# The products that complete a solve, alternating between the two directions of the scan

## Chip, cores and metric

The kernel runs on one core of one Trainium2 chip. The metric is the device time of one execution in microseconds (us): 3263.63 us is the median of three runs before the change (3262.67 to 3264.2). TensorE (PE in the rows, PEld for its weight loads), VectorE (DVE), ScalarE (ACT), GpSimd (POOL) and the DMA queues work side by side and wait for each other by semaphores.

## What is computed

Two layer stacks after each other on 512 tokens of width 1024 in fp32: a gMLP layer and an RWKV layer, each followed by a mixture of experts, then a sliding-window/dilated attention layer and a latent attention layer. The change lies in the RWKV layer's scan, which runs over 256 context tokens and 512 tokens, in two directions, for 16 heads of 64:

```python
def _wkv_step(S, inp):
    r_t, w_t, k_t, v_t, a_t, b_t = inp
    sa = jnp.einsum('zbhvk,zbhk->zbhv', S, a_t)
    S = S * w_t[..., None, :] + sa[..., :, None] * b_t[..., None, :] + v_t[..., :, None] * k_t[..., None, :]
    return S, jnp.einsum('zbhvk,zbhk->zbhv', S, r_t)

def wkv_bidir(state0, scan_in):
    state, ys = lax.scan(_wkv_step, state0, scan_in)
    ys = jnp.moveaxis(ys, 0, 2)
    return state, ys[0] + ys[1][:, ::-1]
```

## The kernel before

**The scan.** `rwkv_scan` works on 8 pairs of heads (`KD` = 8, index c), and cuts the 768 tokens into 12 chunks of 64 (`NCH` = 12, `C` = 64). Index z is the direction, h the head of the pair. Inside a chunk the steps are a triangular system, so its inverse has to be found: for each c a **solve** finds it for all 12 chunks, both directions and both heads at once. Then the **chain** (`Chain.period`) goes through the 12 chunks of the pair, one chunk a period, and carries the state from one to the next.

**A solve.** `scan_decay` and `scan_scaled` prepare its operands: decays and scaled keys in `BK` (line 1363 and 1369) and `AD` (line 1366), of which there are two copies each, used in turn by even and odd c, and 32 by 32 blocks of the system in `MT` (diagonal blocks) and `MO` (off-diagonal blocks). `solve` (line 1415 on) inverts the diagonal blocks on VectorE in 31 steps of two operations (`sol`, `Xx`), and writes the result in two layouts, `XR` (line 1436) and `XL` (line 1437), and parts of it into `XF` (line 1443). The off-diagonal block of the inverse is the product of three 32 by 32 blocks: `solve_v` forms the first product (tile `pv`, copied to `Vs`), `solve_x` the second (tile `px`, copied to `XF`). Both call `products`.

**`products`** holds, for each half b of the 12 chunks, one tile `ps` of one PSUM bank with 6 chunks. For every chunk and direction there is one fp32 matmul: 32 partitions in, 64 columns of weights, 64 moving columns. In `pv` the operands of direction 0 stand on partitions 0 to 31 and those of direction 1 on 64 to 95; in `px` on 32 to 63 and 96 to 127. Direction 0 writes partitions 0 to 63 of the bank, direction 1 partitions 64 to 127. So a call has 24 matmuls in four groups of 6 (half 0 direction 0, half 0 direction 1, half 1 direction 0, half 1 direction 1), and the trace has two records for each, 48 in all. When a half is done, ScalarE copies it out in four copies (line 1461).

**A period of the chain.** Its stages are `py` (tile `pY`), `pg` (`pG`), `pa` (`pA`), `ps` (`pS`) and `pz`, each for another chunk ahead; in the trace a period of one of the later 8 chunks of a pair is 36 records from `pY` to `pz`.

**What sets the order.** `todo` in `rwkv_scan` says before which period each step of the next pair's preparation is written: `solve` one period before the pair's first chunk is through, `solve_v` at its ninth period and `solve_x` at its tenth. Within one engine a scheduler orders the instructions by a simulated time line; the chain's matmuls, and from solve 1 on those of `products`, go through `R.pe = ch.pe`, an `Ordered` engine, whose instructions keep the order in which they are written. In solve 0, before the chain begins, `R.pe` is the plain engine.

**After the scan** come the RWKV layer's output projection (`rwkv_out`), a router that sorts the tokens for the second mixture of experts (`moe`; weights `we`, `wx` by the SyncE queue), the attention layer (`swa`) and the latent attention layer (`mla`).

Of the kernel before, what the change touches and what calls it, by code (L numbers as in the profile page):

```python
# [1445 lines left out]
def q(b):  # L1446
    return slice(32 * b, 32 * b + 32)


def products(K, R, name, lhs, rhs, out):  # L1450

    nh = NCH // 2
    for b in range(2):
        ps = R.q.tile([P, nh, 2, 32], F32, name=name, tag=R.tq[1 - b], bufs=2 if b else R.nq)
        for z in range(2):
            for i in range(nh):
                j = b * nh + i
                R.pe.matmul(ps[z * C:(z + 1) * C, i], lhsT=lhs(z, j), rhs=rhs(z, j), start=True, stop=True)
        for z in range(2):
            for h in range(2):  # L1460
                K.nc.scalar.copy(out(z, h, slice(b * nh, (b + 1) * nh)), ps[q(2 * z + h), :, h, :])
# [6 lines left out]
def solve_v(K, R, c, S):  # L1468

    S.V = V = R.s4.tile([P, NCH, 2, 32], F32, name="Vs")  # L1470
    products(K, R, "pv", lambda z, j: S.MO[q(2 * z), 2 * j:2 * j + 2].rearrange("p h t -> p (h t)"), lambda z, j: pair(S.XR, 2 * z, j),
             lambda z, h, js: V[q(2 * z + 1), js, h])


def solve_x(K, R, c, S):

    products(K, R, "px", lambda z, j: S.V[q(2 * z + 1), j].rearrange("p h t -> p (h t)"), lambda z, j: pair(S.XL, 2 * z + 1, j),
             lambda z, h, js: S.XF[q(2 * h), z, js, q(2 * h + 1)])
# [930 lines left out]
```

## Time and profile before

| | |
|---|---|
| median of three runs | 3263.63 us |
| the profiled execution | 3263.15 us |
| its span, first to last instruction | 3261.3 us |
| mean granted TensorE clock in it | 0.948 |
| TensorE busy | 2975.5 us, 91% of the span |
| VectorE busy | 1507.1 us, 46% |
| ScalarE busy | 1029.7 us, 32% |
| the scan, first `pv` to the last `pY` | 1437.06 to 2069.9 us |

All rows come from the one profiled execution; times in them are microseconds from the start of its span. A busy engine is one with an instruction in flight, so overlapping matmuls count once; several matmul records can be in flight at the same time. The granted clock is given as a share of 2.4 GHz: 1.00 is 2.4 GHz and 0.50 is 1.2 GHz. In the names, `pv<-XR,MO` is an instruction that writes `pv` and reads `XR` and `MO`; numbers of buffers are left out.

### The profile page before, as it was taken

What the parts mean: (1) busy time and instruction counts of PE and PEld (TensorE: products, weight loads), DVE (VectorE), ACT (ScalarE), POOL (GpSimd) and SP (SyncE); (2) the same over time, 40 slices, a digit from 0 to 9 for tenths busy, and PEclk for the clock granted to TensorE, in tenths of its full rate; (3) what the DMA queues carried; (4) which work ended last, traced back from release to release, by engine and by line L of the source; (5) the groups of instructions that cost most, each with busy time, mean ns of one, the idle gap of its engine ahead of it and who ended that gap; (6) DMA issues with size and microseconds to landing.
All of it is one profiled execution on the core that took longest, in us unless ns stands there. A gap on an engine that the chain in (4) does not pass through costs nothing. (4 is left out here: it accounts for less than half of the span.)

```text
span 3261.3 us, 51448 instructions
## 1 busy us (share of the span) xinstructions
PE 2975.5 (91%) x19312; PEld 2105.7 (65%) x19312; DVE 1507.1 (46%) x3441; ACT 1029.7 (32%) x2318; POOL 369.5 (11%) x456
## 2 busy tenths in 40 slices
PE   8999997999999799967999999889999978899998
PEld 4777786555545378646777778755554536777866
DVE  4342345010000399677787885441111125665584
ACT  4111231111111343254555554310000014544463
POOL 1022323111111100000000000021111110000000
PEclk9999998999999899978898999989999998999999
DMA  7545515899999814121111101569999993221200
GB/s 282 183 174 199 203 49 223 294 408 407 406 405 405 312 63 145 58 75 33 38 39 38 39 23 37 193 272 400 408 407 405 403 342 122 59 71 66 72 33 33
DMA packets 222834, 637.66 MB, mean 196 GB/s; under 512 B 37778, under 2 KB 65250, under 8 KB 222448
## 3 DMA queue, kind: packets, MB, share of 16 engines
q1 hardware_dynamic: 180048, 565.13, 45.6%
q10 hardware_dynamic: 27472, 45.72, 4.2%
q0 software_dynamic: 15056, 23.41, 2.0%
q8 instruction: 156, 2.56, 0.3%
q14 instruction: 102, 0.84, 0.1%
HBM read 609.24 MB, written 49.00 MB: 202 GB/s over the span
## 5 line engine op out<-in xcount | busy, mean ns | idle before, releaser
L793 ACT ACTIVATE hg<-pg 128x256 f32<-128x256 f32 x86 | 33.0, 383 | 787.1 <-PE pg L1495 787.1
L794 DVE TENSOR_TENSOR hg<-hg,pu 128x256 f32<-128x256 f32 x86 | 36.2, 421 | 521.0 <-PE pu L1495 518.3
L71 DVE TENSOR_TENSOR wl<-wr,wh 128x1024 fp32r<-128x1024 f32 (+1 forms) x140 | 168.5, 1219 | 121.2 <-ACT wh L70 120.4
L141 PE MATMUL ps<-hT,wh 128*128 128x512 f32 (+1 forms) x496 | 188.3, 380 | 8.4 <-DVE q L1957 3.8
L142 PE MATMUL ps<-hT,wh 128*128 128x512 f32 (+1 forms) x496 | 183.8, 371 | 0.0
L143 PE MATMUL ps<-hT,wl 128*128 128x512 f32 (+1 forms) x496 | 183.6, 371 | 0.0
L70 ACT CAST wh<-wr 128x1024 fp32r<-128x1024 f32 (+1 forms) x140 | 141.3, 1041 | 126.3 <-PE ps L143 43.3
L1495 PE MATMUL pu<-wx,xT 128*64 128x256 f32 x1520 | 176.3, 380 | 4.7 <-DMA wx<-in_moe_wu 4.7
L1495 PE MATMUL pd<-wx,hT 128*64 128x512 f32 x704 | 161.8, 598 | 16.5 <-issue 6.8
L1495 PE MATMUL pg<-wx,xT 128*64 128x256 f32 x1520 | 174.2, 379 | 1.1 <-DMA wx<-in_moe_wg 0.9
L764 DVE COPY hT<-pth 128x128 f32<-128x128 f32 x86 | 25.1, 291 | 312.3 <-ACT hT L763 308.6
L1495 PE MATMUL pd<-we,hT 128*64 128x512 f32 x672 | 154.8, 599 | 13.3 <-issue 8.4
L1495 PEld LDWEIGHTS pu<-wx,xT 128*64 128x64 f32 x1520 | 110.2, 137 | 83.9 <-issue 25.3
L734 POOL DMA_INDIRECT xe<-hrow,idx x86 | 88.3, 1026 | 652.5 <-PE ptr L1495 610.4
L1495 PE MATMUL pu<-we,xT 128*64 128x256 f32 x1232 | 143.2, 380 | 6.2 <-DMA we<-in_moe_wu 6.2
L1495 PE MATMUL pg<-we,xT 128*64 128x256 f32 x1232 | 144.9, 385 | 2.7 <-ACT xT L746 1.2
L1495 PEld LDWEIGHTS pg<-wx,xT 128*64 128x64 f32 x1520 | 111.5, 137 | 55.0 <-issue 2.1
L158 POOL TENSOR_TENSOR rs_r<-rs_t,nhalf 128x1 f32<-128x1 f32 (+2 forms) x52 | 45.5, 877 | 788.1 <-DVE rs_t L156 727.4
L1495 PEld LDWEIGHTS pu<-we,xT 128*64 128x64 f32 x1232 | 88.8, 137 | 66.6 <-issue 16.4
L1495 PE MATMUL pG<-SCB,Zx 128*128 128x128 f32 (+1 forms) x768 | 119.0, 303 | 12.4 <-DVE SCB L1562 8.5
L1495 PEld LDWEIGHTS pg<-we,xT 128*64 128x64 f32 x1232 | 90.1, 139 | 50.6 <-issue 5.4
L1495 PEld LDWEIGHTS pG<-SCB,Zx 128*128 128x128 f32 x768 | 104.8, 211 | 18.9 <-ACT Zx L1572 8.3
(583 smaller groups left out, 6545.0 us busy)
## 6 DMA issues: line engine op xcount, KB each, us to landing
wx<-in_moe_wu SPq DMA_DIRECT2D x144, 512.0 KB
wx<-in_moe_wg SPq DMA_DIRECT2D x144, 512.0 KB
wx<-in_moe_wd SPq DMA_DIRECT2D x130, 512.0 KB
we<-in_moe_wd SPq DMA_DIRECT2D x126, 512.0 KB
we<-in_moe_wg SPq DMA_DIRECT2D x112, 512.0 KB
we<-in_moe_wu SPq DMA_DIRECT2D x112, 512.0 KB
w<-in_ada_w SPq DMA_DIRECT2D x96, 512.0 KB
wr<-in_ga_w_in SPq DMA_DIRECT2D x32, 512.0 KB
```

The costliest lines, as they stand in the source:

```text
L70: nc.scalar.copy(hi, x)
L71: nc.vector.tensor_tensor(out=lo, in0=x, in1=hi.bitcast(F32), op=OP.subtract)
L141: nc.tensor.matmul(ps, lhsT=a[0], rhs=b[0], start=start, stop=False, **kw)
L142: nc.tensor.matmul(ps, lhsT=a[0], rhs=b[1], start=False, stop=False, **kw)
L143: nc.tensor.matmul(ps, lhsT=a[1], rhs=b[0], start=False, stop=stop, **kw)
L158: nc.gpsimd.tensor_tensor(out=r, in0=t, in1=K.nhalf[:, :n], op=OP.pow)
L734: nc.gpsimd.indirect_dma_start(out=xe[i % 3], out_offset=None, in_=hhalf, in_offset=bass.IndirectOffsetOnAxis(ap=idx[:, u, 0, r:r + 1], ax ...
L764: nc.vector.tensor_copy(hT[:, 1], pt[:, 1])
L793: nc.scalar.activation(hg, pg, AF.Silu)
L794: nc.vector.tensor_tensor(out=hg, in0=hg, in1=pu, op=OP.mult)
L1495: r = f(*a, **kw)
```

## The change

In `products` the loop over the two directions becomes the inner one: for each chunk the matmul of direction 0 and then that of direction 1 are issued. The matmuls, their operands and the copies are the same.

```diff
     for b in range(2):
         ps = R.q.tile([P, nh, 2, 32], F32, name=name, tag=R.tq[1 - b], bufs=2 if b else R.nq)
-        for z in range(2):
-            for i in range(nh):
-                j = b * nh + i
+        for i in range(nh):
+            j = b * nh + i
+            for z in range(2):
                 R.pe.matmul(ps[z * C:(z + 1) * C, i], lhsT=lhs(z, j), rhs=rhs(z, j), start=True, stop=True)
         for z in range(2):
             for h in range(2):
```

On TensorE the call stands at the same place. These are the rows around the `pv` and the `px` of one solve in the changed kernel; those of the kernel before read word for word the same (a row groups instructions of one name, x24 being the 24 matmuls of a call):

```order
L1495 MATMUL pz<-SC_11277,XF_9952 128x128 x2
L1495 MATMUL pv<-XR,MO 64x64 x24
L1495 MATMUL pY<-SV,G 128x64 x4
L1495 MATMUL pG<-SCB,Zx_10662 128x128 x4
...
L1495 MATMUL pz<-SC_11316,XF_9952 128x128 x2
L1495 MATMUL px<-XL,Vs 64x64 x24
L1495 MATMUL pY<-SV,G 128x64 x4
```

Nothing moved between the rows; what is new is the order within the two rows of 24.

On VectorE the first difference comes after the scan, in the router of the second mixture of experts (`ptr` is a transposed token tile, `h2T` its copy, `lg` the logits, the other names are small steps of the sorting):

```order
 L416 CAST grp<-gi 128x3
-L394 COPY h2T<-ptr 128x512
 L417 TENSOR_TENSOR oh<-i_16786,grp 128x12
 L420 TENSOR_TENSOR el<-lg,oh 128x32 x3
 L422 TENSOR_REDUCE es<-el 128x24
+L394 COPY h2T<-ptr 128x512
 L425 MAX em<-es 128x8 x3
 L426 MAX_INDEX ei<-em,es 128x8 x3
```

The copy of the last token tile now stands behind the five small operations instead of ahead of them.

On TensorE the first difference comes in the attention layer, where projection matmuls (`ps`), scores (`pss`), transposes of the probabilities (`pt`) and their products with the values (`po`) are interleaved. Before:

```order
L1974 MATMUL pss<-kb,q 128x256 x8
L141 MATMUL ps<-hT,wh 128x512
...
L2068 MATMUL po<-PT,vb_21225 64x128 x6
L2054 MATMUL pt<-ident,e 128x128 x5
L1974 MATMUL pss<-kb,q 128x256 x8
L2054 MATMUL pt<-ident,e 128x128 x3
L142 MATMUL ps<-hT,wh 128x512
```

And with the change:

```order
L1974 MATMUL pss<-kb,q 128x256 x4
L143 MATMUL ps<-hT,wl 128x512
L1974 MATMUL pss<-kb,q 128x256 x4
L2054 MATMUL pt<-ident,e 128x128
L2068 MATMUL po<-PT,vb_21225 64x128 x6
L2054 MATMUL pt<-ident,e 128x128 x7
L141 MATMUL ps<-hT,wh 128x512
```

The scores are cut into groups of four around a projection matmul, and the transposes stand together.

## Rows read from the trace of the kernel before

**Rows 1.** Windows: length; busy (instructions) of PE PEld DVE ACT POOL; granted clock; DMA.

```profile
1520.00:1600.00 80.00, 72.29 (x604) 60.66 (x604) 64.36 (x144) 45.70 (x118) 3.84 (x6) 0.91 0.13 39
...
1995.00:2078.00 83.00, 77.97 (x552) 65.20 (x550) 32.47 (x89) 39.34 (x102) 3.65 (x7) 0.92 0.18 62
```

**Rows 2.** Waits in the scan: who on whom, us in total, times, longest.

```profile
PE pv L1495 <- DVE XR L1436: 30.6, 6, 11.5
...
DVE BK L1363 <- PE pS L1495: 22.7, 6, 4.5
...
DVE AD L1366 <- PE pA L1495: 17.6, 6, 3.3
```

**Rows 3.** Timeline of TensorE in solve 2: start, us, instruction, records, [idle before].

```profile
1600.21 4.44 PE L1495 MATMUL pv<-XR,MO 32*64 32x64 f32 x48 [4.14 <-DVE XR L1436]
1604.58 1.97 PE L1495 MATMUL pY<-SV,G 128*128 128x64 f32 x8
...
1611.41 4.25 PE L1495 MATMUL px<-XL,Vs 32*64 32x64 f32 x48
1615.59 1.74 PE L1495 MATMUL pY<-SV,G 128*128 128x64 f32 x8
```

**Rows 4.** Timeline of VectorE after the px of solve 1.

```profile
1537.41 0.42 DVE L1602 TENSOR_TENSOR SV<-pY,WL 64x256 f32<-64x256 f32 x1 [2.09 <-PE pY L1495]
...
1541.95 0.96 DVE L1363 SCALAR_TENSOR_TENSOR BK<-ta,L 128x768 f32<-128x768 f32 x1 [3.51 <-PE pS L1495]
```

**Rows 5.** The SyncE queue right after the scan, then a window of the experts.

```profile
2068.13 8.99 SPq L130 DMA_DIRECT2D wr<-in_rw_wo  x4
...
2300.00:2400.00 100.00, 93.51 (x712) 55.59 (x708) 15.12 (x35) 9.18 (x27) 17.32 (x17) 1.00 1.03 408
```

**Rows 6.** TensorE's groups in the scan: records, busy us, mean ns, idle before.

```profile
L1495 PE MATMUL pv<-XR,MO 32*64 32x64 f32 x336 | 30.9, 290 | 30.6 <-DVE XR L1436 30.6
L1495 PE MATMUL px<-XL,Vs 32*64 32x64 f32 x336 | 29.7, 284 | 0.0
```

**Rows 7.** Timeline, pieces of the pv of solve 1: start, us, records.

```profile
1520.48 0.51 PE L1495 MATMUL pv<-XR,MO 32*64 32x64 f32 x3
...
1521.15 0.58 PE L1495 MATMUL pv<-XR,MO 32*64 32x64 f32 x6
...
1521.04 0.69 PE L1495 MATMUL pv<-XR,MO 32*64 32x64 f32 x7
```

**Rows 8.** Windows of 10 ns in that pv: the first (x) is records in flight.

```profile
1520.75:1520.76 0.01, 0.01 (x3) 0.01 (x2) 0.00 (x0) 0.50 0.00 0
...
1521.40:1521.41 0.01, 0.01 (x5) 0.01 (x4) 0.00 (x0) 0.50 0.00 0
```

**Rows 9.** Timeline of TensorE before the loop: the px of solve 0.

```profile
1443.52 4.44 PE L1458 MATMUL px<-XL,Vs 32*64 32x64 f32 x48 [2.04 <-ACT Vs L1461]
```

**Rows 10.** Timeline of ScalarE after the pv of solve 1.

```profile
1525.39 2.58 ACT L1461 COPY Vs<-pv 32x192 f32<-32x192 f32 x8
```

**Rows 11.** Windows, one period each: after px (two of seven), undisturbed, sum after pv.

```profile
1536.27:1542.53 6.26, 6.26 (x35) 4.92 (x35) 1.58 (x4) 2.33 (x7) 0.00 (x0) 0.73 0.26 86
1615.59:1623.45 7.86, 7.86 (x36) 6.49 (x36) 1.58 (x4) 2.34 (x7) 0.00 (x0) 0.57 0.23 69
...
2042.90:2047.44 4.54, 4.54 (x36) 3.88 (x35) 1.13 (x3) 2.47 (x8) 0.00 (x0) 1.00 0.12 33
...
sum 50.73, PE 50.73 PEld 41.26 DVE 14.63 ACT 33.31 POOL 0.00; mean PE 7.25 PEld 5.89 DVE 2.09 ACT 4.76 POOL 0.00
```

**Rows 12.** Windows of the px of solve 1 and of what follows it.

```profile
1532.10:1536.20 4.10, 4.10 (x49) 3.99 (x48) 3.16 (x5) 2.27 (x8) 0.00 (x0) 1.00 0.00 0
1536.20:1541.00 4.80, 4.80 (x23) 3.40 (x22) 1.00 (x3) 1.26 (x5) 0.00 (x0) 0.64 0.34 113
```

**Rows 13.** Timeline of VectorE in the router.

```profile
2144.88 0.69 DVE L394 COPY h2T<-ptr 128x512 f32<-128x512 f32 x1 [0.86 <-PE ptr L393]
```

**Rows 14.** Window of the attention layer, the first of three alike.

```profile
2700.00:2800.00 100.00, 93.43 (x432) 76.80 (x433) 57.98 (x170) 44.52 (x114) 3.14 (x6) 0.93 0.28 87
```

## Prediction

> **What bounds the kernel now.** I read the work per stretch first, then who waited for whom in the scan, then the order of time around two solves. In one head pair of the scan [rows 1] TensorE is busy 72.29 of 80.00 us and VectorE 64.36; in the last stretch 77.97 of 83.00 and 32.47. No engine alone fills the stretch, so the waits decide. They run in both directions [rows 2]: TensorE stands before `pv` until VectorE's `XR` is there (6 times, 30.6 us), and VectorE stands before `AD` until TensorE has read the old `pA` operands (17.6 us) and before `BK` until `pS` is through (22.7 us, 6 times). That is one ring: solve on VectorE, `pv`, one period of the chain, `px`, one more period, then `BK` on VectorE and the next solve. [Rows 3] shows TensorE's half of it without a gap: `pv` from 1600.21, `pY` at 1604.58, `px` at 1611.41, `pY` at 1615.59, and no idle time from there to the next `pY` at 1623.45 [rows 11]. A microsecond taken from TensorE there lets VectorE start `BK` one microsecond earlier; VectorE had been idle 2.09 and 3.51 us there [rows 4], so it can follow. After the last solve nothing waits for VectorE, and TensorE runs without gaps to the end of the scan.
>
> What follows moves along. The output projection's weights are asked for at 2068.13 [rows 5], after the scan, and the experts' weights later still; the experts run at the memory's pace (408 GB/s with all DMA engines busy). Nothing there started before the scan was over, so an earlier end of the scan is an earlier end of the kernel.
>
> **Part 1: the products.** Each call of `products` is 24 fp32 matmuls, 48 records, 4.37 us to the next instruction for `pv` and 4.18 for `px` [rows 3]; seven calls of each are busy 30.9 and 29.7 us [rows 6]. In the present order six matmuls (12 records) of one direction follow each other and then six of the other. The two directions read other partitions (0-31 and 64-95 in `pv`, 32-63 and 96-127 in `px`) and write the two halves of one bank. Within a direction three records are in flight [rows 8], and 3 records take 0.51 us; with 0.28 for one [rows 6], that is (0.51 - 0.28) / 2 = 0.115 us from start to start [rows 7]. That pace is not the clock's: `pv` ran at a granted 0.50 [rows 8] and `px` at 1.00 [rows 12], and their lengths differ by 4%. But where the order changes direction (at about 1521.15, and again at 1522.1 and 1523.1) five records are in flight [rows 8], and 6 records take 0.58 us: (0.58 - 0.28) / 5 = 0.060. There the last records of one direction and the first of the other run side by side, each at its own pace. The first of these places is inside one bank, so two writers of one bank do not exclude each other there. Each call has three such changes now; that is why it takes 4.2 and not 48 x 0.115 = 5.5 us.
>
> In the new order every second matmul is of the other direction, so this state should last the whole call. Two streams of 24 records at 0.115: 2.76 us. Saved: 4.37 - 2.76 = 1.61 per `pv` and 4.18 - 2.76 = 1.42 per `px`. Bounds: if every record came at 0.055 (two streams at 0.11), 2.64 us a call, 1.73 and 1.54 saved; if the pace stayed that of the mixed stretch of 7 records in 0.69 us, (0.69 - 0.28) / 6 = 0.068, 3.26 a call, 1.11 and 0.92 saved. I take 2.76, nearest to the row where both streams are certainly running.
>
> Solves 1 to 7: 7 x (1.61 + 1.42) = 21.2 us (bounds 14.2 and 22.9). Solve 0 stands before the loop: there `px` waits 2.04 us for the copies to `Vs` [rows 9], which stand on ScalarE behind four copies from `XL`, so a faster `pv` buys nothing; `px` is faster by the same 1.4, but ScalarE copies its result before `tw`, for which the next steps wait, and those copies keep their length, so I count 1.0 (0.5 to 1.5). Sum: 22.2 us, bounds 14.7 and 24.4.
>
> What is late next? Between `pv` and `px` ScalarE copies `Vs` from 1525.39 to 1527.97 [rows 10]; the `px` of that solve started at about 1532.1 [rows 12], and would want to start 1.6 us earlier, at about 1530.5, so the copies still hide. Semaphores, DMAs and copies of the call stay as they are.
>
> **Part 2: the clock.** The same 36 records of one period (`pY` to `pz`) take 4.54 us at a granted clock of 1.00, but 6.26 (five times) or 7.86 us (twice) after `px`, and 7.25 on the mean after `pv` [rows 11]. In solve 1 the granted clock was 1.00 during `px` and 0.64 on the mean of the 4.8 us behind it [rows 12]: its two levels are 1.00 (2.4 GHz) and 0.50 (1.2 GHz). In all seven solves the engine fell to the lower level around the end of `px`, though it had not been idle; it had done nothing but these small matmuls for 4.18 us. The excess after `px` is 5 x (6.26 - 4.54) + 2 x (7.86 - 4.54) = 15.2 us; after `pv` 50.73 - 7 x 4.54 = 19.0 us. With a thin stretch of 2.76 instead of 4.18 us some of the falls after `px` should not come. How many, no row tells; the ends are none (0) and all (15.2), and I take half, 7.6 us, since a third of the thin stretch goes. The stretch after `pv` follows a wait of about 4 us that stays as it is, so I take 0 there, with 9.5 as the far end; it could also lengthen a little, since the clock may come back no earlier while `pv` ends earlier: 5 us at worst.
>
> **Part 3: what else moves.** On all four engines the rows up to the end of the scan stand as before. Behind it the scheduler, which works with its own clock, breaks some ties in another way. In the router one copy moves behind five small operations, which can fill a wait of 0.86 us [rows 13]: under 1 us either way. Among the experts the weights set the pace [rows 5]. In the attention layer TensorE is idle 100 - 93.43 = 6.6 us in the first of three windows [rows 14], some 18 in all three; transposes and scores exchanged with projection matmuls can move a few of these, I take 0 with 5 to either side.
>
> **Sum.** 22.2 + 7.6 = 29.8 us off. The profiled execution took 3263.15 us (its span 3261.3), 0.48 below the median of the runs shown; 3263.15 - 29.8 = 3233.4, so I forecast 3233.
>
> **Rivals.**
> (a) The clock is given back everywhere: 24.4 + 15.2 + 9.5 = 49 us off, 3214, or a little less. For it: the falls follow exactly the thin stretches. Against: the wait before `pv` remains.
> (b) The streams run side by side only in part, and the clock gives nothing: 14.7 off, 3248. For it: the trace shows overlaps of a few records only, at a change of direction.
> (c) The ring is VectorE's alone: what TensorE saves comes back as a longer wait before `pv`. Then only the last solve, where nobody waits, is faster: about 3 us, 3260, no change that a measurement could tell (it tells about 0.2%, 6.5 us). Against it: `AD` and `BK` wait for TensorE in every solve.
> (d) Slower: two matmuls that write one bank shut each other out, and the overlap at the changes is something else (the next bank). Then the alternation loses the three overlaps that there are: 48 x 0.115 = 5.52 us a call, 7 x (1.15 + 1.34) = 17.4 us more, 3281; if each change also pays a new start, more. It decides if the pace of an alternating call is above 4.37 / 48 = 0.091 us a record. Against it: the five in flight at 1521.40 are 12 records after the call's start, within the first bank.
>
> On (d) there is a rule: the Trainium skill, TensorEngine Tiling, section Restrictions and Gotchas, says under PSUM pressure that different row tiles write different banks and cannot access the same bank at the same time. By it the time would be that of (d). The trace disagrees at the first change of a call [rows 8]: there the rule costs nothing that can be seen.
>
> That the change does nothing is not likely: the matmuls of solves 1 to 7 carry the chain's order, so the scheduler cannot put them back.
>
> **How the numbers follow.** Likeliest (3216 to 3243): 0.65. (a): 0.08. (b): 0.11. (c): 0.09. (d): 0.07. Faster by over 0.2%: 0.65 + 0.08 + 0.11 = 0.84; within: 0.09; slower: 0.07. The range reaches from (a)'s 3214 to (b)'s 3248, one more for the attention layer: 3214 to 3249, which leaves out (c), (d) and half of (a), 0.20.
>
> **What would show it.** In the profile after: `pv` and `px` busy about 19 us each over seven calls instead of 30.9 and 29.7, four to six records in flight throughout; the wait of `pv` for `XR` unchanged at about 4 us (if it grows by 3, it is (c)); the period after `px` at 4.54 us in some solves. Wrong it would be with a call above 3.3 us, or with the scan shorter and the attention layer longer.

## The result, and the profile after

| | before | after |
|---|---|---|
| median, five runs each side by side | 3263.63 us | 3226.93 us |
| lowest and highest of them | 3262.42 to 3270.09 | 3226.0 to 3228.85 |
| span of the profiled execution | 3261.3 us | 3225.1 us |
| mean granted TensorE clock | 0.948 | 0.950 |
| scan, start of the first `pv` to start of the last `pY` | 632.60 us | 597.63 us |

The ratio is 0.9888, with a 95% interval of 0.9878 to 0.9899: 36.7 us faster. The forecast was 30 us faster, 3233, in a range of 3214 to 3249. Nearly all of it lies in the scan, 35.0 of the 36.2 us by which the span is shorter. From the end of the scan to the end of the kernel 1.7 us are gained, and the first `pv` starts 0.5 us later.

TensorE's groups in the scan, of the kernel after (records, busy us, mean ns of one, idle time before), against [rows 6]. The last row is the `px` of solve 0:

```profile
L1495 PE MATMUL pv<-XR,MO 32*64 32x64 f32 x336 | 20.3, 287 | 30.6 <-DVE XR L1436 30.6
L1495 PE MATMUL px<-XL,Vs 32*64 32x64 f32 x336 | 20.0, 283 | 0.0
...
L1458 PE MATMUL px<-XL,Vs 32*64 32x64 f32 x48 | 2.9, 287 | 3.6 <-ACT Vs L1461 3.6
```

The records are as long as before, 287 and 283 ns. They only overlap more: 30.9 us of `pv` became 20.3, and 29.7 of `px` became 20.0. The wait ahead of `pv` is what it was, 30.6 us.

The timeline of TensorE in solve 2, after, against [rows 3]:

```profile
1595.37 2.90 PE L1495 MATMUL pv<-XR,MO 32*64 32x64 f32 x48 [4.14 <-DVE XR L1436]
1598.19 1.97 PE L1495 MATMUL pY<-SV,G 128*128 128x64 f32 x8
...
1605.77 2.86 PE L1495 MATMUL px<-XL,Vs 32*64 32x64 f32 x48
1608.55 1.10 PE L1495 MATMUL pY<-SV,G 128*128 128x64 f32 x8
```

From `pv` to the next instruction it is 1598.19 - 1595.37 = 2.82 us (4.37 before), from `px` 2.78 (4.18 before). In the last row there is a second change: the eight records of `pY` behind `px` take 1.10 us where [rows 3] has 1.74. Behind `pv` they take 1.97 as before.

Windows of 10 ns in the `pv` of solve 1, after (length, TensorE's busy time and, in brackets, records in flight, granted clock, DMA share and GB/s), against [rows 8]:

```profile
1519.60:1519.61 0.01, 0.01 (x3) 0.50 0.00 0
1521.00:1521.01 0.01, 0.01 (x5) 0.50 0.00 0
1521.50:1521.51 0.01, 0.01 (x6) 0.50 0.00 0
```

After the start, five or six records are in flight at every one of these points, where before it was three, and five only at a change of direction.

Windows of the period after `px`, after: solve 1, then solves 2 and 7, and the sum of all seven, against [rows 11] (length; busy time and records of PE, PEld, DVE, ACT and POOL; granted clock; DMA share; GB/s):

```profile
1533.03:1538.72 5.69, 4.81 (x36) 3.98 (x35) 2.73 (x7) 3.26 (x10) 0.00 (x0) 1.00 0.31 95
1608.55:1613.20 4.65, 4.65 (x36) 3.98 (x35) 2.02 (x6) 2.40 (x8) 0.00 (x0) 1.00 0.39 116
1974.73:1979.38 4.65, 4.65 (x37) 3.99 (x36) 1.30 (x4) 2.40 (x8) 0.00 (x0) 1.00 0.11 32
...
sum 33.59, PE 32.71 PEld 27.90 DVE 13.90 ACT 17.62 POOL 0.00; mean PE 4.67 PEld 3.99 DVE 1.99 ACT 2.52 POOL 0.00
```

The granted clock is 1.00 throughout, where before it fell in all seven solves. The seven periods took 5 x 6.26 + 2 x 7.86 = 47.0 us and take 33.6 now. In solve 1 the period holds 0.88 us of idle time (5.69 - 4.81), which is new.

The same for the stretches between `pv` and `px`: two of the seven and their sum:

```profile
1897.83:1905.76 7.93, 7.93 (x37) 6.44 (x35) 3.98 (x8) 6.79 (x18) 0.57 (x2) 0.57 0.00 0
1965.60:1971.94 6.34, 6.34 (x37) 5.33 (x35) 2.35 (x7) 5.61 (x14) 0.00 (x0) 0.73 0.00 0
sum 51.98, PE 51.98 PEld 42.10 DVE 25.20 ACT 44.91 POOL 3.42; mean PE 7.43 PEld 6.01 DVE 3.60 ACT 6.42 POOL 0.49
```

Here nothing was given back: 50.7 us before, 52.0 now, and the clock is at its lower level for much of the time.

The waits in the scan, after, against [rows 2] (who on whom, us in total, times, longest). The last row is from the kernel before:

```profile
DVE AD L1366 <- PE pA L1495: 19.4, 6, 3.4
DVE SV L1602 <- PE pY L1495: 17.4, 25, 3.4
DVE BK L1363 <- PE pS L1495: 11.4, 6, 1.9
...
DVE SV L1602 <- PE pY L1495: 39.6, 26, 4.8
```

VectorE now waits 11.4 us ahead of `BK` instead of 22.7, and 17.4 us for `pY` instead of 39.6. The three waits together are 48.2 us where they were 79.9: they shrink by 31.7 us, about what TensorE saved in solves 1 to 7 (32.5 us, added up below).

### The profile page after: what moved, and what is told of

The parts are those of the page before. It is cut to its first block, busy times and chain, and to the rows that moved or that the text cites. A ratio compares the mean times of both kernels' runs of the same rounds, so it can differ in the third digit from the quotient of the medians.

```text
span 3225.1 us, 51447 instructions
## 1 busy us (share of the span) xinstructions
PE 2943.8 (91%) x19309; PEld 2085.9 (65%) x19312; DVE 1507.8 (47%) x3441; ACT 1032.5 (32%) x2318; POOL 367.9 (11%) x456
## 5 line engine op out<-in xcount | busy, mean ns | idle before, releaser
L794 DVE TENSOR_TENSOR hg<-hg,pu 128x256 f32<-128x256 f32 x86 | 36.2, 421 | 523.0 <-PE pu L1495 514.2
L1495 PEld LDWEIGHTS pd<-wx,hT 128*64 128x64 f32 x704 | 48.1, 136 | 105.2 <-issue 75.8
```

Of the source, the lines that this page charges most:

```text
L794: nc.vector.tensor_tensor(out=hg, in0=hg, in1=pu, op=OP.mult)
L1495: r = f(*a, **kw)
```

## The experiments

A step is "alternated" below if its matmuls stand as in the changed kernel. "The period after `px`" runs from the first `pY` behind `px` to the next `pY`; "after `pv`" means up to the `px` that follows. "A fall" is a change of the granted clock from 1.00 to 0.50. The names `S.AD`, `K.ident` and `R.mL` are operands that are there anyway: the solve's `AD`, the identity and a mask.

### One product alternated, the other not

```diff
-        for z in range(2):
-            for i in range(nh):
...
+        turns = [(z, i) for i in range(nh) for z in range(2)] if name == "pv" else [(z, i) for z in range(2) for i in range(nh)]
+        for z, i in turns:
```

and the same with `"px"`. Expected for `pv` alone:

> Only the first product (pv) alternates; px goes direction by direction as before. If the two streams run side by side and the clock after px is px's own affair: pv 2.83 us a call, px 4.18, the period after px 6.3 to 7.9 us as before, time 3263.6 - 7 x 1.54 = about 3253. If the clock's gain came from the alternation anywhere in the solve (a shorter pv too): the period after px is 4.65 in most solves, and the time is below 3245.

and for `px` alone:

> Only the second product (px) alternates; pv goes direction by direction. Side by side and the clock px's own: px 2.79 us, pv 4.37, the period after px 4.65 in nearly all solves, time 3263.6 - 7 x 1.39 - 13 = about 3240, a little less for solve 0. If pv's share were the larger: above 3248. The gains of the two halves should add up to about 36 us if they do not depend on each other.

Measured: `pv` alone 3255.84 us, ratio 0.9967 (0.9952 to 0.9981), scan 12.0 us shorter than before; `px` alone 3241.28 us, 0.9921 (0.99 to 0.9941), scan 22.7 us shorter. The two sum to 34.7 of the changed kernel's 35.0 in the scan, so they don't interact much. The period after `px` in solve 2, first with `pv` alone, then with `px` alone:

```profile
1618.50:1624.76 6.26, 6.26 (x36) 5.25 (x36) 1.59 (x4) 2.34 (x7) 0.00 (x0) 0.73 0.30 86
```

```profile
1610.36:1615.21 4.85, 4.81 (x36) 3.98 (x35) 2.23 (x6) 2.53 (x9) 0.00 (x0) 1.00 0.39 112
```

With `px` left at 4.18 us the clock falls behind it in all seven solves; with `px` at 2.79 it falls in none, and the seven periods sum to 33.3 us. So `px` is worth twice as much as `pv`, though both lose about the same time: 7 x 1.39 = 9.7 us of its own, and 47.0 - 33.3 = 13.7 us of clock behind it.

### Is it the density of the small matmuls, or how long they last?

Each matmul of `px` is written twice, alternated, so its records come as densely as in the changed kernel, but for twice as long.

```diff
-                R.pe.matmul(ps[z * C:(z + 1) * C, i], lhsT=lhs(z, j), rhs=rhs(z, j), start=True, stop=True)
+                for n in range(2 if name == "px" else 1):
+                    R.pe.matmul(ps[z * C:(z + 1) * C, i], lhsT=lhs(z, j), rhs=rhs(z, j), start=True, stop=True)
```

> Both alternate, but every matmul of px is issued twice, with the same result: px has 96 records, at 0.058 us 5.6 us a call, longer than the 4.18 of before, and as dense as the new order. If the falls of the clock after px are a matter of how long only such small matmuls run: they are back in all seven solves, the period after px is 6.3 to 7.9 us, the time 3226.9 + 8 x 2.8 + 13 = about 3262. If they are a matter of how dense the matmuls are: the period stays at 4.65, the time is about 3249.

Measured: 3265.22 us, ratio 1.0003 (0.999 to 1.0016). Solve 1's `px` and the period behind it:

```profile
1530.69:1536.15 5.46, 5.46 (x97) 5.29 (x96) 2.88 (x5) 2.06 (x7) 0.00 (x0) 1.00 0.21 72
1536.15:1544.01 7.86, 7.86 (x36) 6.49 (x35) 1.87 (x5) 2.33 (x7) 0.00 (x0) 0.57 0.06 19
```

At the same 0.057 us a record the longer stretch brings the fall back, in all seven solves (in two of them before `px` is over). Density alone doesn't keep the clock up. The other way round: the order of before, with `px`'s two halves in two periods.

```diff
-            for i, (at, f) in enumerate(((-2, scan_scaled), (-1, solve), (1, scan_r), (8, solve_v), (9, solve_x))):
+            for i, (at, f) in enumerate(((-2, scan_scaled), (-1, solve), (1, scan_r), (8, solve_v), (9, solve_x1), (10, solve_x0))):
```

> The kernel before, direction by direction, but px's two halves stand in two periods of the chain (chunks 6 to 11 in the ninth, 0 to 5 in the tenth), about 2.1 us each with a period between them. If the falls after px come from the length of the stretch of small matmuls: no or few falls without any alternation, periods of 4.6 us behind both, time 3263.6 - 13 = about 3250. If the alternation's density is what keeps the clock: falls after one or both halves, 3260 or more.

Measured: 3258.85 us, ratio 0.9979 (0.9969 to 0.999). A first half and the period behind it, in solve 1 and in solve 2:

```profile
1540.55:1542.91 2.36, 2.36 (x26) 2.19 (x25) 2.33 (x3) 0.89 (x3) 0.00 (x0) 1.00 0.00 0
1542.91:1547.65 4.74, 4.74 (x35) 3.96 (x35) 2.35 (x7) 2.43 (x7) 0.00 (x0) 1.00 0.39 114
1618.77:1621.13 2.36, 2.36 (x25) 2.19 (x24) 2.30 (x4) 0.82 (x3) 0.00 (x0) 1.00 0.00 0
1621.13:1629.08 7.95, 7.95 (x36) 6.46 (x35) 2.13 (x6) 2.43 (x7) 0.00 (x0) 0.57 0.22 68
```

Behind 5 of the 14 halves the clock fell, against 7 of 7 whole calls. A shorter stretch helps even at the old pace, but not always. Four of the five began 0.8 to 1.0 us after the clock had come back from an earlier fall; of the ten that began later after it, the clock fell behind one. So when a stretch begins counts as well as its length. The halves also cost 2 x 2.36 - 4.18 = 0.54 us more a solve. Each expectation was met in part.

### Does sharing a bank cost anything?

The two directions write into two banks at any time, each into its own half.

```diff
+    ps = [R.q.tile([P, nh, 2, 32], F32, name=name, tag=R.tq[1 - b], bufs=2 if b else R.nq) for b in range(2)]
...
-                R.pe.matmul(ps[z * C:(z + 1) * C, i], lhsT=lhs(z, j), rhs=rhs(z, j), start=True, stop=True)
+                j = (b ^ z) * nh + i
+                R.pe.matmul(ps[b ^ z][z * C:(z + 1) * C, i], lhsT=lhs(z, j), rhs=rhs(z, j), start=True, stop=True)
```

> Alternating as in the changed kernel, but direction 0 and direction 1 write different banks at any moment (direction 0 of one half beside direction 1 of the other half). If two writers of one bank cost each other nothing: 2.8 us a call as in the changed kernel, 3227 within 3. If sharing the bank slows them: a call below 2.7 us, and a time lower by 14 calls x the difference. The copies of the first half start later, which the trace of the changed kernel says is hidden.

Measured: 3234.52 us, ratio 0.9903 (0.988 to 0.9927). Its products in the scan:

```profile
L1496 PE MATMUL pv<-XR,MO 32*64 32x64 f32 x336 | 20.2, 285 | 30.6 <-DVE XR L1436 30.6
L1496 PE MATMUL px<-XL,Vs 32*64 32x64 f32 x336 | 20.0, 283 | 0.0
...
L1458 PE MATMUL px<-XL,Vs 32*64 32x64 f32 x48 | 4.8, 289 | 3.8 <-ACT Vs L1462 3.8
```

The same 20.2 and 20.0 us as with one bank, so that costs nothing here. Solve 0's `px` is longer (4.8 us), since the copies to `Vs` can't start before both banks are done. The time missed the 3227 that was expected. In the profiled execution the first `pv` started 3.7 us later than in the changed kernel, ahead of anything that this edit touches, and from there to the `pv` of solve 1 it took 5.2 us more; the rest of the scan was 2.4 us shorter.

### How far ahead does TensorE look?

Three matmuls (six records) of a direction, then three of the other.

```diff
-        for i in range(nh):
+        for i in [i for g in (0, 3) for z in range(2) for i in ((z, g), (z, g + 1), (z, g + 2))]:
+            z, i = i
             j = b * nh + i
-            for z in range(2):
-                R.pe.matmul(ps[z * C:(z + 1) * C, i], lhsT=lhs(z, j), rhs=rhs(z, j), start=True, stop=True)
+            R.pe.matmul(ps[z * C:(z + 1) * C, i], lhsT=lhs(z, j), rhs=rhs(z, j), start=True, stop=True)
```

> Directions alternate every three matmuls (6 records) instead of every one. If the engine can begin the other direction while two or three records of the first still wait their turn: most of the overlap stays, a call takes about 3.0 us (two records ahead) to 2.9 (three), against 2.8 for every one and 4.2 to 4.4 for every six, and the clock stays up after px: about 3230. If the overlap needs the very next matmul to be of the other direction: a call of 3.8 to 4.2 us, falls after px, about 3255.

Measured: 3232.53 us, ratio 0.9905 (0.9882 to 0.9929). Solve 2:

```profile
1598.52 3.15 PE L1495 MATMUL pv<-XR,MO 32*64 32x64 f32 x48 [4.14 <-DVE XR L1436]
1601.60 1.97 PE L1495 MATMUL pY<-SV,G 128*128 128x64 f32 x8
...
1608.38 3.11 PE L1495 MATMUL px<-XL,Vs 32*64 32x64 f32 x48
1611.41 0.77 PE L1495 MATMUL pY<-SV,G 128*128 128x64 f32 x5
```

3.08 and 3.03 us a call in this solve, between 2.8 (every matmul) and 4.2 to 4.4 (every six). How fast one stream goes by itself shows in six records of one direction in the `px` of solve 1 of the kernel before, at a granted 1.00:

```profile
1532.33 0.84 PE L1495 MATMUL px<-XL,Vs 32*64 32x64 f32 x6
```

That is (0.84 - 0.28) / 5 = 0.112 us from start to start, so 48 records of one stream would take 5.38 us. The three changes of direction in a call of before hid (5.38 - 4.18) / 3 = 0.40 us each; the seven here hide (5.38 - 3.05) / 7 = 0.33 each, the time of three to four records. The starts of the records say the same: at the first change in [rows 7] the second direction begins at 1521.155, when nine of the first direction's twelve records have started. So TensorE reaches past the stream that it is held by, but only some three records far.

### Which difference lets them overlap: the rows read, or the half written?

In `pv` and `px` both differ at once. In a wait ahead of the first `pv`, where TensorE has nothing else to do, stand series of 24 such matmuls of their own. They add work and change no result (one run each, 3231.2 and 3229.8 us). First the rows differ and the half doesn't (partitions 0-31 and 64-95 are read, all results go to partitions 0-63, but into two banks in turn), then only the half (one group of rows, the halves of one bank in turn):

```diff
+    for t, (rows, halves, banks) in enumerate(((2, 0, 2), (0, 1, 1))):
...
+            g, o = q(z * rows), z * halves * C
+            R.pe.matmul(ps[z % banks][o:o + C, n // 2 % 6], lhsT=K.ident[g, :C], rhs=K.ident[g, C:], start=True, stop=True)
```

> The changed kernel with two trials of 24 matmuls each in TensorE's wait of 17 us before the pv of solve 0 (their results are not used). First: operands alternate between partitions 0-31 and 64-95, all write partitions 0-63, of two banks in turn. Second: all operands on partitions 0-31, results alternate between partitions 0-63 and 64-127 of one bank. If the partitions read are what makes two streams: the first takes 2.8 us, the second about 5.3. If the partitions written are: the first 5.3, the second 2.8. If both are needed: 5.3 each. If either is enough: 2.8 each.

```profile
1411.78 2.48 PE L1476 MATMUL trial<-ident 32*64 32x64 f32 x48 [0.72 <-ACT ro L1174]
1414.20 1.22 PE L1511 MATMUL pA<-BK,AD 128*128 128x128 f32 x4
...
1423.11 2.82 PE L1476 MATMUL trial<-ident 32*64 32x64 f32 x48 [1.09 <-ACT junk L1479]
1425.86 1.22 PE L1511 MATMUL pA<-BK,AD 128*128 128x128 f32 x4
```

Both overlap: 2.42 and 2.75 us to the next instruction, at a mean granted clock of 0.59 and 0.50. As this could also come from the series' own operands, a control: same rows and same half with a contiguous and with a strided moving operand, then same rows and alternating halves, strided.

```diff
+    for t, (halves, strided) in enumerate(((0, 0), (0, 1), (1, 1))):
...
+            o = n % 2 * halves * C
+            rhs = R.mL[q(0), 0].rearrange("p (t h) -> p h t", h=2) if strided else K.ident[q(0), C:]
+            R.pe.matmul(ps[o:o + C, n // 2 % 6], lhsT=K.ident[q(0), :C], rhs=rhs, start=True, stop=True)
```

> Control for the two trials of rows and halves: in the wait before solve 0's pv stand three series of 24 small matmuls, all from the same 32 partitions. First: the results in one half of the bank, moving operand contiguous. Second: the same with the moving operand strided as in pv and px. Third: results alternating between the halves, strided. If the overlap needs either other rows or another half, the first and the second take 48 x 0.115 = 5.5 us and the third 2.8. If the contiguous operands alone made the trials fast, the first takes 2.8 and the second 5.5. If the stride alone costs, the third takes 5.5 too. The extra work lies in a wait; time as the changed kernel's within 6 us.

```profile
1410.71 5.08 PE L1476 MATMUL trial<-ident 32*64 32x64 f32 x48 [0.72 <-ACT ro L1174]
1415.59 5.32 PE L1476 MATMUL trial<-mL,ident 32*64 32x64 f32 x48
1420.84 1.22 PE L1510 MATMUL pA<-BK,AD 128*128 128x128 f32 x4
...
1423.49 2.83 PE L1476 MATMUL trial<-mL,ident 32*64 32x64 f32 x48
1426.24 1.22 PE L1510 MATMUL pA<-BK,AD 128*128 128x128 f32 x4
```

With the same rows and the same half the series takes 4.88 and 5.25 us to the next instruction, 0.10 and 0.11 a record; with another half alone 2.75. So another half alone is enough. Other rows are enough together with two banks in turn; what two banks do by themselves, with the same rows and the same half, was not tried.

The control says less about the stride than was expected of it. Its strided operand steps by 2 elements, those of `pv` and `px` by 32, so it isn't strided as they are. And the clock fell from 1.00 to 0.50 early in the first series, the contiguous one. Its windows before and behind the fall (length, TensorE's busy time and records, granted clock, DMA share and GB/s):

```profile
1410.71:1411.05 0.34, 0.34 (x6) 1.00 0.00 0
...
1411.10:1415.59 4.49, 4.49 (x46) 0.50 0.38 120
```

The first 6 of the 48 records start within 0.34 us, one every 0.057; the other 42 within 4.49, one every 0.107. So this one contiguous stream goes with the clock, and at the full clock it is as fast as the two alternating streams of `px`, where one stream of `px` takes 0.112 a record. The 0.4 us between the first two series hold for the lower level alone. Whether a contiguous operand would have let `pv` and `px` run that fast without any alternation was not tried, nor were two contiguous streams at the full clock for a whole call.

### Can the clock behind pv be kept as well?

First the wait ahead of `pv` is filled with dense matmuls of 384 columns, whose result `pv` overwrites: 14 in solve 1, 4 in solves 2 to 6, none in solve 7, which doesn't wait.

```diff
+        for l, r in warm if b == 0 else ():
+            R.pe.matmul(ps.rearrange("p i h t -> p (i h t)"), lhsT=l, rhs=r, start=True, stop=True)
...
+             [(K.ident, S.AD[:, 0, :3].rearrange("p c h t -> p (c h t)"))] * n)
```

> The changed kernel with useless matmuls (128 partitions, 384 columns, about 0.7 us each) into the bank of pv before pv begins, while TensorE waits for XR: 14 in solve 1, 4 in solves 2 to 6, none in 0 and 7; pv overwrites them. If the wait of about 4 us is what takes the clock down before pv: the granted clock is 1.00 in pv, the period after pv goes from 7.3 to 8.0 us towards 4.65 in solves 1 to 6, the time 3226.9 - 6 x 2.9 = about 3210. If pv itself takes it down: unchanged at about 3227, or a little above.

Measured: 3227.66 us, ratio 0.9887 (0.9871 to 0.9904). Solve 2, `pv` behind its filled wait, and the stretch behind it:

```profile
1597.33:1600.12 2.79, 2.79 (x49) 2.67 (x49) 2.74 (x3) 1.00 (x2) 0.93 (x1) 0.86 0.00 0
1600.12:1607.66 7.54, 7.54 (x36) 6.05 (x34) 3.76 (x8) 6.56 (x17) 0.60 (x2) 0.60 0.00 0
```

The clock is now up in most of `pv` (0.86 in solve 2, 0.75 to 0.99 in solves 1 to 6). It falls 0.1 to 1.4 us before the end of `pv`, and the stretch behind takes 7.3 to 7.9 us, as before; nothing is gained. The first of the two expected outcomes, a clock that stays up, did not come: the fall doesn't need the wait. The fillers leave 1.2 to 2.5 us of the wait idle in solves 1 to 5, but only 0.33 of 2.90 us in solve 6, and it fell there too. Next, the fillers get dense weights in place of the identity, which is nearly all zeros:

```diff
-             [(K.ident, S.AD[:, 0, :3].rearrange("p c h t -> p (c h t)"))] * n)
+             [(S.AD[:, 0, 0].rearrange("p h t -> p (h t)"), S.AD[:, 0, :3].rearrange("p c h t -> p (c h t)"))] * n)
```

> The matmuls that fill the wait before pv hold the solve's own operand AD as weights in place of the identity, which is nearly all zeros; nothing else differs from the run that filled the wait with the identity (3227.7 us, clock lost after pv in all seven solves). If the zeros made those fillers count for little, the stretch after pv shortens from about 7.4 us towards 4.6 in most solves and the time is 3205 to 3215. If pv itself takes the clock down, whatever stood ahead of it, the stretch after pv stays at 7.3 to 7.9 us and the time at 3225 to 3231.

Measured: 3226.03 us, ratio 0.9882 (0.9865 to 0.9899), the same. The stretch behind `pv` in solve 2 again:

```profile
1600.90:1608.01 7.11, 7.11 (x36) 5.87 (x35) 3.76 (x8) 6.37 (x17) 0.62 (x2) 0.65 0.00 0
```

So the zeros weren't it either. Last, two of these dense matmuls also stand between the halves of `pv`, and two ahead of it in solve 7:

```diff
-        for l, r in warm if b == 0 else ():
+        for l, r in warm if b == 0 else warm[:2]:
...
-    n = {1: 14, 7: 0}.get(c, 4) if c else 0
+    n = {1: 14, 7: 2}.get(c, 4) if c else 0
```

> As the run with AD as weights, and two such dense matmuls (0.64 us each at the full clock, by the columns that the fillers had) stand also between the two halves of pv, so that no thin stretch of the call is longer than 1.4 us. They cost 2 x 0.64 x 7 = 9 us. If pv's own thin stretch takes the clock down, the falls after pv go: 7 x (7.4 - 4.6) = 20 us back, 3215 to 3218 in all, and the period after pv reads 4.6 us. If the clock falls for another reason, the period after pv stays at 7.3 to 7.9 us and the time is 3236.

Measured: 3242.04 us, ratio 0.9925 (0.9902 to 0.9949), 16 us slower than with the dense fillers alone; its runs lie wider apart than the others' (3232.0 to 3245.3), and the profiled one, from which the counts below come, is the slowest of them. The filled wait with `pv`, the stretch after it, `px` and the period after `px`, in solve 5; then the first two of these and the last in solve 2:

```profile
1830.58:1838.95 8.37, 7.15 (x63) 4.58 (x61) 7.96 (x16) 3.45 (x7) 1.54 (x2) 1.00 0.01 4
1838.95:1843.69 4.74, 4.74 (x37) 3.96 (x35) 2.22 (x5) 4.54 (x13) 0.00 (x0) 1.00 0.00 0
1843.69:1846.48 2.79, 2.79 (x50) 2.62 (x49) 2.73 (x4) 2.64 (x10) 0.00 (x0) 1.00 0.00 0
1846.48:1852.74 6.26, 6.26 (x37) 5.04 (x35) 2.02 (x6) 2.39 (x8) 0.00 (x0) 0.73 0.29 86
1598.54:1607.91 9.37, 7.81 (x62) 4.77 (x60) 8.26 (x17) 4.12 (x7) 1.54 (x2) 0.85 0.00 0
1607.91:1616.14 8.23, 8.23 (x36) 6.74 (x35) 2.77 (x5) 4.58 (x16) 0.00 (x0) 0.55 0.00 0
...
1618.93:1623.58 4.65, 4.65 (x37) 3.99 (x36) 1.59 (x4) 2.39 (x8) 0.00 (x0) 1.00 0.38 113
```

In five solves (1, 4, 5, 6 and 7) the stretch after `pv` takes 4.74 us at full clock, as hoped: in 5, 6 and 7 the clock doesn't fall in or behind `pv`, in 1 and 4 it falls inside the call and is back before the call ends. But in these five the clock falls behind `px`, which is the same 2.79 us as in the changed kernel; in solves 2 and 3, where it falls in `pv` and is down behind it, it doesn't fall behind `px`. Over seven solves the stretches after `pv` give 13.3 us back (38.7 against 52.0), the periods after `px` take 7.0 (40.5 against 33.6), and the waits with `pv` grow by 17.3 (67.7 against 50.4, the fillers that don't fit into the wait among it). That is 11 us lost, as the scan shows (609.3 against 597.6).

## Why the prediction was right, and where it was off

| step | predicted | measured |
|---|---|---|
| `pv` and `px`, solves 1 to 7 | -21.2 (-14.2 to -22.9) | -20.3 |
| solve 0 | -1.0 | -1.3 |
| clock after `px` | -7.6 (0 to -15.2) | -13.4 |
| clock after `pv` | 0 (+5 to -9.5) | +1.3 |
| rest of the scan | 0 | -1.2 |
| outside the scan | 0 (5 either way) | -1.2 |
| sum | -29.8 | -36.2 |

The measured terms are read from the two profiled executions and rounded one by one; solve 0 runs from the first `pv` to the `pv` of solve 1.

**The products: right.** 2.76 us a call was forecast; 2.83 for `pv` (2.79 in solve 7) and 2.79 for `px` came. Saved are 1.54 in most calls of `pv` and 1.39 in `px`, 20.3 us in seven solves. Rival (b), a partial overlap at 3.26 us a call, is out with that. The step that carried it was to read the pace of two streams from the places where the order changes direction. The records in flight are five to six (four to six forecast), and the record's own length is what it was.

**The ring: right.** `pv` waits the same 30.6 us for `XR`; if VectorE alone set the pace (c), this would have grown by what was saved. VectorE's waits for TensorE shrink instead, by 31.7 us. One reading of the prediction was a little off: the output projection's weights were asked for at 2068.13, 1.5 us before the last `pY` starts and not after the scan. No term of the sum rests on it.

**Shared bank, rival (d): wrong, as the first change of direction had shown.** One bank or two, a call takes 2.8 us. The Trainium skill, TensorEngine Tiling, section Restrictions and Gotchas, says that different row tiles cannot access the same PSUM bank at the same time; for two that write different halves the runs here disagree, at 20.2 us with two banks against 20.3 with one.

**The clock after `px`: the mechanism was right, the size was not.** This is the term that was mis-sized: half of the falls were counted (7.6 us), all of them went (13.4). "Half, since a third of the thin stretch goes" had no row behind it. The runs replace it by counts. Behind a `px` of 4.2 us (before, and `pv` alone) the clock fell 14 times of 14, in or behind 5.5 us 7 of 7, behind 3.0 us 1 of 7, behind 2.8 us 0 of 7 in the changed kernel and 0 of 42 in the six other runs with the same `px` and nothing dense inside `pv`. The length alone doesn't decide: behind the halves of 2.36 us, at the old pace, it fell 5 times of 14. The far end of 15.2 was not reached, since the period at full clock is 4.65 and not 4.54 us, and solve 1's is 5.69, with idle time in it. With 13.4 for 7.6 the forecast would have been 3227.6; the median is 3226.9.

**But the count has a condition that no expectation had.** In the changed kernel each `px` starts 1.1 to 2.5 us after the clock came back from the fall around `pv`. In the run with dense matmuls inside `pv` the clock had been up for 6 us or more, and the same 2.79 us took it down, five times of five. It isn't a rule: in the run with threes the clock had been up for 67 us ahead of solve 7's `px`, and stayed up. In the first run with series of small matmuls it had been up for 26 us ahead of solve 7's `px`, and stayed up too. The stretch after `pv` and the period after `px` in that solve:

```profile
1969.81:1974.55 4.74, 4.74 (x36) 3.96 (x34) 2.05 (x6) 4.58 (x12) 0.00 (x0) 1.00 0.01 3
...
1977.34:1981.99 4.65, 4.65 (x37) 3.99 (x35) 1.30 (x4) 2.46 (x8) 0.00 (x0) 1.00 0.10 28
```

So it may be that falls after `px` went because the falls around `pv` stayed, as the run with dense matmuls inside `pv` suggests, but that isn't shown. Rival (a), the clock given back everywhere, came about in no whole run; in solve 7 of these two runs both falls were gone at once.

**The clock after `pv`: right to count nothing.** It got 1.3 us worse, inside the 5 named. Why the clock falls there is not settled. The wait ahead is not needed for it (nearly filled in solve 6, absent in solve 7), zeros in the fillers are not the cause, and with dense work in the middle of `pv` the fall came behind `px` in each solve whose stretch after `pv` ran at full clock. The call itself doesn't decide either: in solve 7, behind the same `pv` of 2.79 us without a wait, the clock fell in the changed kernel and stayed up in the run with `px` doubled and in the rows above. What fixes the moment of a fall was not tried by itself.

**The rest.** Solve 0 gave 1.3 us (1.0 forecast): its `px` waits 3.6 us for `Vs` instead of 2.0, so the faster `pv` bought nothing there, as said. The 1.2 us in the rest of the scan and the 1.2 outside were not followed further.

## What to carry to other kernels

Where small matmuls of two tiles stand in two blocks, alternate them one by one: 48 records that took 4.2 us in blocks of six matmuls take 2.8. Another half of the results is enough for it; other rows were enough with two banks in turn. Compare the pace with that of a contiguous operand at the full clock first (0.057 us a record here): this kernel may have had a second way to the same 2.8 us, which was not tried. Look for the places where the order changes already: their records in flight tell the gain before the edit. Then read the granted clock of the dense stretch behind such a block; shortening the block was worth more there (13.4 us) than in `px` itself (9.7), and filling a wait to keep the clock was worth nothing here.

## What the hardware showed that was not expected

- The same rows are no hindrance. Matmuls that read the same 32 partitions and write alternating halves of one bank run side by side: 2.75 us against 5.25 in one half. The Trainium skill, TensorE: Matmul & The Clock Gate, section Part 3: Packing small matmuls, says that a weight load overlaps running matmuls only where the row group differs; the traces here disagree, since with the same rows a record started every 0.057 us (2.75 / 48) where the half alone differed, and in the control's first series, with one half, a load from 1410.76 to 1410.89 lies inside a matmul from 1410.71 to 1410.97 (the ends of matmuls are modelled).
- The pace of `pv` and `px` is not set by the clock: 2.83 us for `pv` at a granted 0.50, 2.79 for `px` at 1.00. That of matmuls of the same size on a contiguous operand is: 0.057 us a record at 1.00 and 0.107 at 0.50 in one stream. The step of the operand, 32 elements against 1, is the difference that stands out; it wasn't tried by itself at the full clock.
- TensorE lost its clock without an idle moment, behind 4.2 and 5.5 us of small matmuls, and in solve 7 of the changed kernel behind a `pv` of 2.8 us with no wait ahead of it (0.73 on the mean of the stretch from 1965.60).
- Filling the wait ahead of `pv` raised the clock inside `pv` from 0.50 to between 0.75 and 0.99 and shortened it by 0.04 us only (2.83 to 2.79): the small matmuls hardly need it, and the work behind them paid as before.
